# The down projection of an encoder layer: its operands made a third of a pair at a time, its partial sums loaded two at a time

## The chip, the cores and the metric

The kernel runs on one core of one Trainium2 chip. The metric is the device time of one execution in microseconds (us); less is better. The core has TensorE for matmuls (PE in the profile, its weight loads PEld), VectorE (DVE), ScalarE (ACT), GpSimd (POOL) and SyncE (SP); the last two and ScalarE also issue DMA transfers. Each engine works through its own queue in order, so an instruction that waits holds up all those behind it on the same engine.

## The reference

One layer of a hybrid encoder on a sequence of 512 tokens, width 2048, in float32. Behind a mixing stage (dilated attention and gated linear attention, not touched here) stands a SwiGLU with a hidden width of 5632:

```
h = rmsnorm(x, ffn_norm_w[l])
x = x + (jax.nn.silu(h @ w_gate[l]) * (h @ w_up[l])) @ w_down[l]
...
return rmsnorm(x, final_norm_w)
```

The change lies in the last product, by w_down (5632 x 2048).

## The kernel before

**Split operands.** A float32 operand is carried as two parts: `hi`, rounded by a cast on ScalarE, and `lo`, the rest, a subtraction on VectorE. Each product then takes three matmuls: hi x hi, hi x lo, lo x hi. So every weight that comes from memory costs a cast and a subtraction before TensorE can use it.

**Products of pairs.** A block of 2 x 2 tiles is multiplied by a scheme with seven products in place of eight. On the weights it needs sums (L1089 to L1091, VectorE), then the split of the loaded part and of the sums (casts L1101, subtractions L1106, two each). On the activations it needs, for each pair of 128-row tiles, sums and differences (L1323 to L1326) and their splits (L1335 to L1339, four casts and four subtractions). These are "the operands of a pair". The generator `operands` makes them and yields three times for each pair: behind L1326, behind the second split, and behind the fourth. So `make(1)` puts out a third of a pair and `make(3)` a whole one. A pair counts as made only with the call behind its last third, which begins the next pair too. The pair's raw tile is loaded by L1309 on SP from `gd`, where the gate and up stage had stored the activations; it starts a third only if enough buffers are free.

**Stages of w_down.** The 44 row tiles are dealt with in this order; the output has four blocks of 512 columns (c = 0 to 3):

1. Tiles 0 to 3 by plain products: four jobs, one for each block, of four halves each; a half is 12 matmuls of 512 columns (L293 to L295). Its weights are split at L196 and L197, three halves ahead. Before each half `before_down` runs (L1268), which calls `dn.make(3)`. Each job's result is added into `xd` in memory (L1262 on ScalarE, L1264 on POOL). In front of it `down_start` has made the first call of the generator, which loads two raw tiles.
2. Pairs 2 to 17 by the seven products (`Down`, L1286): 64 steps, ordered by chunk of pairs (2 to 7, 8 to 12, 13 to 17), within a chunk by block, within a block by pair. A step is 42 matmuls of 256 columns (L1374 to L1376), seven products of six. The pairs of a chunk are kept for its four blocks and their buffers are freed in its fourth. `run` (L1440) puts out, for step i: the load of weights (L1073, SP), the sums of step i + 2, the split of step i + 1, results that are still to be stored, then, while the step's pair is not made, `make(1)`; then the products, then `make(2)` and one call of `run_urgent`, which advances the first generator in the deque `urgent` to its next yield. At the last step of a block in a chunk the seven results go to `md` in memory: in the first chunk by plain stores from SP (L1398), later by adding stores from POOL (L1396).
3. When the last chunk has finished a block, `combine` (L1408) is put in `urgent`. It loads the block's seven sums from `md` (L1411, SP) and four tiles of the residual from `xd` (L1414, POOL), and some calls later adds them up in VectorE (L1422 to L1431) and into the residual (L1434).
4. Tiles 36 to 39 by plain products again: four jobs of four halves, 16 in all (`before_later`, L1474). A job's results are added to the residual by L1254, which frees the PSUM banks. Their splits run ever further ahead, so that at the end the weights of the next stage are split too. `run_side` advances `urgent` once behind each half but a job's last.
5. Tiles 40 to 43, the residual, the final norm and the stores (`finish`, L1514), in 16 groups of 12 matmuls (L1547 to L1549); `drain` ahead of it finishes whatever `urgent` still holds.

The order on each engine is the order in which the program puts instructions out; nothing reorders them. Buffers come from deques `s2` (70 of 512 columns), `s4` (16 of 1024) and `ps` (8 PSUM banks), the longest free one first, and whoever takes a buffer waits for its last reader.

Of the kernel before, what the change touches and what calls it, by code (L numbers as in the profile page):

```python
# [111 lines left out]
def put(*slots):  # L112
    for s in slots:
        if s.home is not None:
            s.home.free.append(s.i)


def layer(nc, tc, x, attn_norm_w, w_in, rel_table, gw_f, gb_f, gw_b, gb_b, gla_norm_w, w_out,
# [7 lines left out]
    with tc.manual_schedule(), \  # L126
# [5 lines left out]
        s2 = Slots(p2, N2, 512, "a")  # L132
# [22 lines left out]
        class Stream:  # L155
# [11 lines left out]
            def add(self, pieces):  # L167

                for segs in pieces:
                    self.pieces.append([segs, None])  # L170
                    for h in range(2):
                        self.halves.append([len(self.pieces) - 1, h, None, None])
# [52 lines left out]
        def run_urgent():  # L225
            while urgent:
                try:
                    next(urgent[0])
                    break
                except StopIteration:  # L230
                    urgent.popleft()
# [709 lines left out]
        x1 = {}  # L941
# [170 lines left out]
        class Feed(Blocks):  # L1112
# [80 lines left out]
            def run(self):  # L1193
                banks = {}
                for i, (u, q) in enumerate(self.seq):
                    if u not in banks:
                        banks[u] = [ps.get() for _ in range(4)]
                    self.load()
                    self.split(i)
                    self.sums(i + 1)  # L1200
                    self.sums(i + 2)
                    self.split(i + 1)
                    self.products(i, banks[u])
                    if u == len(self.units) - 1:
                        for p in (2 * q, 2 * q + 1):
                            put(*xs.pop(p)["slots"])
                        down_start(q)
                    for _ in range(3 if i < 8 else 1):
                        run_urgent()
                    if q == self.per - 1:  # L1210
                        urgent.append(self.evac(u, banks.pop(u)))
# [7 lines left out]
        def g_load(j):  # L1219
            if j < FF // 256 and j not in graw and 2 * j not in gT and j >= state["g"]:  # L1220
                state["g"] = j + 1
                graw[j] = s4.get(F32, [P, 2, 512])
                sp.dma_start(out=graw[j].t.rearrange("p f t -> p (f t)"), in_=gd[j])

        def g_split(j):
            if j in graw:
                r = graw.pop(j)
                for f in (1, 0):
                    hi, lo = s2.get(F32R), s2.get(F32R)
                    if f:  # L1230
                        act.activation(hi.t, r.t[:, f], AF.Copy, scale=-1.0)
                        dve.scalar_tensor_tensor(lo.t, r.t[:, f], -1.0, hi.f, op0=OP.mult, op1=OP.subtract)
                    else:
                        act.copy(hi.t, r.t[:, f])
                        dve.tensor_tensor(lo.t, r.t[:, f], hi.f, op=OP.subtract)
                    gT[2 * j + 1 - f] = (hi, lo)
                put(r)
# [30 lines left out]
        def before_down(c):  # L1268
            def f(i):
                if c == 0 and i == 0:  # L1270
                    g_split(1)
                dn.make(3)
                if c == 3:
                    dn.load()
                    if i >= 1:
                        dn.sums(i - 1)
                    if i == 2:
                        dn.split(0)
            return f
# [6 lines left out]
        class Down(Blocks):  # L1286
# [120 lines left out]

            def combine(self, c):  # L1408
                m = [s2.get(F32, [P, 2, 256]) for _ in range(7)]
                for n in range(7):  # L1410
                    sp.dma_start(out=m[n].t.rearrange("p s c -> p (s c)"), in_=md[7 * c + n])  # L1411
                x1[c] = [s2.get() for _ in range(4)]
                for t in range(4):
                    pool.dma_start(out=x1[c][t].t, in_=xd[4 * c + t])  # L1414
                for _ in range(3 if c < 3 else 5):
                    yield
                M = [None] + [x_.t for x_ in m]
                y = [s4.get(F32, [P, 2, 512]) for _ in range(2)]
                lo, up = slice(0, 256), slice(256, 512)
                add = lambda o, x_, y_: dve.tensor_tensor(o, x_, y_, op=OP.add)  # L1420
                sub = lambda o, x_, y_: dve.tensor_tensor(o, x_, y_, op=OP.subtract)
                add(y[0].t[:, :, up], M[2], M[1])  # L1422
                sub(M[3], M[1], M[3])
                yield
                sub(M[5], M[5], M[3])
                add(M[3], M[4], M[3])
                yield
                sub(y[0].t[:, :, lo], M[5], M[7])
                add(y[1].t[:, :, up], M[6], M[3])
                yield  # L1430
                sub(y[1].t[:, :, lo], M[5], M[4])  # L1431
                put(*m)
                for t in range(4):
                    dve.scalar_tensor_tensor(x1[c][t].t, y[t // 2].t[:, t % 2], rstd2[:, t:t + 1], x1[c][t].t,  # L1434
                                             op0=OP.mult, op1=OP.add)
                    if t % 2:
                        yield
                put(*y)

            def run(self):  # L1440
                for i, (ch, c, q) in enumerate(self.seq):
                    self.load()
                    self.sums(i)
                    self.split(i)
                    self.sums(i + 1)
                    self.sums(i + 2)
                    self.split(i + 1)
                    self.evac_late()
                    while q not in self.x:
                        self.make(1)  # L1450
                    self.products(i)
                    self.make(2)
                    run_urgent()
                    if ch == len(self.chunks) - 1 and c == 3:
                        n = self.chunks[ch].index(q)
                        if n == 0:
                            g_load(LAST // 2 - 2)
                        if n == 2:
                            g_split(LAST // 2 - 2)
                            g_load(LAST // 2 - 1)  # L1460
                            st.until, st.limit = None, 1
                            st.load()
                        if n > 2:
                            st.split(later_first + n - 2)
                self.evac_late()
                st.limit, st.big = 3, tail_first
# [7 lines left out]
        def before_later(c):  # L1474
            def f(i):
                j = LAST // 2 - 2 + (c + 1)
                if c and i == 0:
                    g_load(j)
                if i == (2 if c else 0) and c < 3:
                    g_split(j)  # L1480
            return f

        LAST = 40
# [11 lines left out]
        for c in range(4):  # L1495
            j = job("B", [piece512(w_down, c * 512, k) for k in (LAST - 4, LAST - 2)], list(range(LAST - 4, LAST)),
                    lambda k: gT[k], evac_later(c), before=before_later(c), rate=1.0)
            j.tail = c
            if c == 3:
                j.drop = drop_g  # L1500
        tail_first = len(st.halves)
        dn = Down([list(range(2, 8)), list(range(8, 13)), list(range(13, 18))])
# [94 lines left out]
```

## Time and profile before

| | us |
|---|---|
| median of 3 runs | 2249.7 |
| the runs | 2247.34 to 2252.29 |
| the profiled execution | 2248.97 |
| its span, first to last instruction | 2247.2 |
| TensorE busy in the span | 2213.8 |
| VectorE busy | 1633.1 |
| ScalarE busy | 1001.7 |
| stage 1 of w_down, first L293 to first L1374 | 1763.06 to 1817.30 |
| stage 2, first L1374 to the next L293 | 1817.30 to 2150.51 |
| stage 4, to the first matmul of stage 5 | 2150.51 to 2194.05 |

The page shows busy time by engine, then the span in 40 slices. Matmuls overlap and their ends are modelled, so busy time on PE is no measure of how much is lost; the distance between the starts of matmuls is. The chain of waits follows, from the last instruction back, what released each instruction; a line of it gives start, duration and what ran. The list of waits gives engine, line, what it waited for, then the total in us, the number of times and the longest one. A row of the table of stretches gives the stretch, its length, the busy time and number of instructions of PE, PEld, DVE, ACT and POOL, the granted clock of TensorE as a share of full speed, the busy share of the DMA engines and GB/s. A timeline gives start, duration, engine, line, what it writes and reads, and how many were merged.

### The profile page before, as it was taken

How to read it: one execution, taken by the hardware profiler on the slowest of the kernel's cores; microseconds unless marked ns; L12 is line 12 of the kernel's file. 1: busy time of each engine (PE TensorE's matmuls, PEld its weight loads, DVE VectorE, ACT ScalarE, POOL GpSimd, SP SyncE). 2: the span in 40 equal slices, each digit the busy share in tenths (PEclk: the TensorE clock that was granted, in tenths of full speed). 3: DMA queues.
4: the chain of work that ended last, by engine and by line, in shares of the span. 5: the costliest groups of instructions: out<-in, count | busy, mean ns of one | idle time of the engine just before them, and what ended most of it. 6: DMA issues, size and time to landing. Idle time of an engine off the chain costs nothing.

```text
span 2247.2 us, 37030 instructions
## 1 busy us (share of the span) xinstructions
PE 2213.8 (99%) x14814; PEld 2038.0 (91%) x14814; DVE 1633.1 (73%) x2717; ACT 1001.7 (45%) x1637; POOL 116.3 (5%) x173
## 2 busy tenths in 40 slices
PE   8999999999999999999999999999999899999998
PEld 6888887888888888999999999999999799999986
DVE  3366665745454446988888888888888877977777
ACT  5344444443444344434444343434444554655452
POOL 0000000000000100000000000000000110032220
PEclk9999999999999999999999999999999999999999
DMA  5525625232323432333333333333333764578993
GB/s 204 157 72 147 184 78 140 82 122 66 96 71 134 141 122 75 113 113 122 113 123 119 116 123 113 123 114 114 129 115 123 246 165 158 201 174 182 267 314 105
DMA packets 211805, 307.78 MB, mean 137 GB/s; under 512 B 15376, under 2 KB 131264, under 8 KB 211633
## 3 DMA queue, kind: packets, MB, share of 16 engines
q1 hardware_dynamic: 192480, 259.37, 35.9%
q0 software_dynamic: 18256, 44.99, 8.5%
q8 instruction: 116, 1.90, 0.3%
q10 hardware_dynamic: 896, 1.06, 0.1%
q14 instruction: 57, 0.46, 0.1%
HBM read 246.58 MB, written 46.20 MB: 130 GB/s over the span
## 4 chain that ended last, share of the span: by engine, by line
PE 92%; DVE 5%; ACT 1%; DMA 1%; issue 1%; SPq 0%; ACTq 0%; DVEq 0%
PE ps L1149 13%; PE ps L1148 13%; PE ps L1147 13%; PE ps L294 6%; PE ps L293 6%; PE ps L295 6%; PE ps L285 5%; PE ps L286 5%; PE ps L287 5%; PE ps L1375 4%; PE ps L1376 4%; PE ps L1374 4%; PE ps L514 1%; DVE b L1106 1%; DVE a L1339 1%; PE ps L841 1%
## 5 line engine op out<-in xcount | busy, mean ns | idle before, releaser
L1149 PE MATMUL ps<-a,b 128*128 128x256 f32 x2464 | 697.7, 283 | 2.9 <-DVE b L1106 2.9
L1147 PE MATMUL ps<-a,b 128*128 128x256 f32 x2464 | 697.4, 283 | 0.0
L1148 PE MATMUL ps<-a,b 128*128 128x256 f32 x2464 | 697.3, 283 | 0.0
L1101 ACT CAST b<-b 128x768 fp32r<-128x768 f32 x480 | 445.5, 943 | 550.8 <-DVE b L1106 318.8
L1106 DVE TENSOR_TENSOR b<-b,b 128x768 fp32r<-128x768 f32 x480 | 509.3, 1088 | 137.7 <-PE ps L1148 62.2
L1149 PEld LDWEIGHTS ps<-a,b 128*128 128x128 f32 x2464 | 473.0, 192 | 3.8 <-DVE b L1106 3.8
L1148 PEld LDWEIGHTS ps<-a,b 128*128 128x128 f32 x2464 | 473.0, 192 | 0.0
L1147 PEld LDWEIGHTS ps<-a,b 128*128 128x128 f32 x2464 | 473.0, 192 | 0.0
L197 DVE TENSOR_TENSOR a<-b,a 128x512 fp32r<-128x512 f32 x292 | 195.0, 686 | 135.8 <-ACT a L196 128.6
L1375 PE MATMUL ps<-b,a 128*128 128x256 f32 x896 | 255.2, 285 | 6.9 <-DVE b L1106 6.9
L1376 PE MATMUL ps<-b,a 128*128 128x256 f32 x896 | 254.3, 284 | 0.0
L1374 PE MATMUL ps<-b,a 128*128 128x256 f32 x896 | 254.2, 284 | 0.0
L196 ACT CAST a<-b 128x512 fp32r<-128x512 f32 x292 | 171.4, 617 | 53.1 <-DMA b<-in_w_in_dram 18.1
L293 PE MATMUL ps<-a,a 128*128 128x512 f32 x464 | 184.5, 398 | 2.5 <-ACT a L196 2.5
L294 PE MATMUL ps<-a,a 128*128 128x512 f32 x464 | 182.1, 392 | 4.4 <-DVE a L197 4.2
L295 PE MATMUL ps<-a,a 128*128 128x512 f32 x464 | 181.6, 391 | 0.0
L1375 PEld LDWEIGHTS ps<-b,a 128*128 128x128 f32 x896 | 172.6, 193 | 8.7 <-DVE b L1106 8.7
L1089 DVE TENSOR_TENSOR b<-b 128x512 f32<-128x512 f32 x240 | 164.0, 683 | 22.4 <-DMA b<-in_w_down_dram 18.5
L1374 PEld LDWEIGHTS ps<-b,a 128*128 128x128 f32 x896 | 172.7, 193 | 0.0
L1376 PEld LDWEIGHTS ps<-b,a 128*128 128x128 f32 x896 | 172.7, 193 | 0.0
L285 PE MATMUL ps<-a,a 128*128 128x512 f32 x416 | 168.3, 405 | 0.0
L286 PE MATMUL ps<-a,a 128*128 128x512 f32 x416 | 163.4, 393 | 0.0
(224 smaller groups left out, 3072.8 us busy)
## 6 DMA issues: line engine op xcount, KB each, us to landing
b<-in_w_gate_dram SPq DMA_DIRECT2D x88, 512.0 KB, 3.4
b<-in_w_up_dram SPq DMA_DIRECT2D x88, 512.0 KB, 3.5
b<-in_w_down_dram SPq DMA_DIRECT2D x88, 512.0 KB, 5.1
b<-in_w_in_dram SPq DMA_DIRECT2D x96, 256.0 KB, 4.4
b<-in_w_in_dram SPq DMA_DIRECT2D x48, 512.0 KB, 3.8
b<-in_w_out_dram SPq DMA_DIRECT2D x32, 512.0 KB, 4.1
md<-a POOLq DMA_DIRECT2D x56, 256.0 KB, 9.1
a<-a SPq DMA_DIRECT2D x96, 128.0 KB, 2.3
```

The costliest lines, as they stand in the source:

```text
L285: mm(o, wh.t[:, c], xh.t, start=first, stop=False)
L293: mm(o, xh.t[:, c], wh.t[:, w], start=first, stop=False)
L294: mm(o, xh.t[:, c], wl.t[:, w], start=False, stop=False)
L295: mm(o, xl.t[:, c], wh.t[:, w], start=False, stop=last)
L1101: act.copy(hi.t, src)
L1106: dve.tensor_tensor(lo.t, src, hi.f, op=OP.subtract)
L1147: mm(o, wh, xh, start=head, stop=False, skip_group_check=True)
L1148: mm(o, wh, xl, start=False, stop=False, skip_group_check=True)
L1149: mm(o, wl, xh, start=False, stop=end, skip_group_check=True)
L1374: mm(o, xh[:, t], wh, start=first and h == 0, stop=False, skip_group_check=True)
L1375: mm(o, xh[:, t], wl, start=False, stop=False, skip_group_check=True)
L1376: mm(o, xl[:, t], wh, start=False, stop=last, skip_group_check=True)
```

## The change

Four edits. In stage 1 one third of a pair is put out before each half where a whole pair was. In the steps one third is put out behind every second step, and behind every step of the fourth block, where two thirds were put out behind each. `combine` takes its buffers, waits a call (except for the last block), loads the sums of `md` two at a time with a call between, then the last one with the residual, and begins to add a call later (two for the last block). In stage 4 `run_urgent` is called once more, before each half.

```
@@ -1269,7 +1269,7 @@ before_down
                 if c == 0 and i == 0:
                     g_split(1)
-                dn.make(3)
+                dn.make(1)
                 if c == 3:
                     dn.load()
@@ -1407,12 +1407,17 @@
             def combine(self, c):
                 m = [s2.get(F32, [P, 2, 256]) for _ in range(7)]
+                x1[c] = [s2.get() for _ in range(4)]
+                if c < 3:
+                    yield
                 for n in range(7):
                     sp.dma_start(out=m[n].t.rearrange("p s c -> p (s c)"), in_=md[7 * c + n])
-                x1[c] = [s2.get() for _ in range(4)]
+                    if n in (1, 3, 5):
+                        yield
                 for t in range(4):
                     pool.dma_start(out=x1[c][t].t, in_=xd[4 * c + t])
-                for _ in range(3 if c < 3 else 5):
+                yield
+                if c == 3:
                     yield
                 M = [None] + [x_.t for x_ in m]
@@ -1449,7 +1454,8 @@ run
                     while q not in self.x:
                         self.make(1)
                     self.products(i)
-                    self.make(2)
+                    if c == 3 or i % 2:
+                        self.make(1)
                     run_urgent()
@@ -1478,6 +1484,7 @@ before_later
                 if i == (2 if c else 0) and c < 3:
                     g_split(j)
+                run_urgent()
             return f
```

More of the change, by code (lines that the diff above doesn't have):

```diff
@@ L1271, in f @@
                     g_split(1)
-                dn.make(3)
+                dn.make(1)
                 if c == 3:
@@ L1409, in combine @@
                 m = [s2.get(F32, [P, 2, 256]) for _ in range(7)]
+                x1[c] = [s2.get() for _ in range(4)]
+                if c < 3:
+                    yield
                 for n in range(7):
                     sp.dma_start(out=m[n].t.rearrange("p s c -> p (s c)"), in_=md[7 * c + n])
-                x1[c] = [s2.get() for _ in range(4)]
+                    if n in (1, 3, 5):
+                        yield
                 for t in range(4):
                     pool.dma_start(out=x1[c][t].t, in_=xd[4 * c + t])
-                for _ in range(3 if c < 3 else 5):
+                yield
+                if c == 3:
                     yield
@@ L1451, in run @@
                     self.products(i)
-                    self.make(2)
+                    if c == 3 or i % 2:
+                        self.make(1)
                     run_urgent()
@@ L1480, in f @@
                     g_split(j)
+                run_urgent()
             return f
```

## The prediction

> **What bounds the kernel now.** I read the first part of the page, then the waits of the stretch from 1740 us on, then single stages. I call the 64 rounds of L1374 to L1376 (42 matmuls each) steps 0 to 63; the 16 rounds of 12 matmuls ahead of them (stage 1) are halves 0 to 15.
>
> ```profile
> PE 2213.8 (99%) x14814; PEld 2038.0 (91%) x14814; DVE 1633.1 (73%) x2717; ACT 1001.7 (45%) x1637; POOL 116.3 (5%) x173
> ```
>
> ```profile
> PE ps L1375 <- DVE b L1106: 6.9, 8, 3.2
> PE ps L294 <- DVE a L197: 4.2, 4, 1.1
> PE ps L293 <- ACT a L196: 2.5, 2, 1.5
> ```
>
> TensorE is the bound; behind the gate stage it waits only for splits of weights. These waits understate the loss (ends are modelled), so I use starts. Without waiting, matmuls start 0.12 us (256 wide) or 0.227 us (512 wide) apart: stage 4, the twin of stage 1 with 192 matmuls, runs from 2150.51 to 2194.05, 43.5 us or 2.72 a half; stage 1 takes from 1763.06 to 1817.30, 54.2. **10.7 us are lost there.** The 2688 matmuls of the steps last from 1817.30 to 2150.51, 333.2 us, against 64 x 5.04 = 322.6: **10.6 us lost**, by starts of steps 0.25 in step 1, 4.4 in 24 to 28, 1.06 in 42 and 43, 4.99 in step 53. The tail loses nothing. So 21.3 us is all that can be won.
>
> Stage 1, in its chain of waits:
>
> ```profile
> 1778.72 0.33 DVE a L1323
> 1779.05 0.34 DVE a L1324
> 1779.39 0.35 DVE a L1325
> ...
> 1779.76 0.42 DVE a L1326
> 1780.19 0.34 DVE a L1336
> 1780.52 1.81 DVE a L1339 x3
> 1782.33 0.60 DVE a L197
> ```
>
> A whole pair of operands (L1323 to L1339) is 3.6 us of VectorE, and the weight split L197, which TensorE waits for, stands behind it: 4.2 us a half against 2.72. Steps 24 to 28 have the same cause. Step 53 has another:
>
> ```profile
> 2072.10 13.15 DMA md<-a
> 2085.26 0.32 SPq L1411
> 2085.69 0.38 SPq L1073
> ...
> 2086.68 5.90 DMA b<-in_w_down_dram
> 2092.59 0.96 DVE b L1106
> 2093.59 0.43 PE ps L1375
> 2070.80 14.78 SPq L1411 DMA_DIRECT2D a<-md  x7
> ```
>
> Seven loads of sums hold SP for 14.8 us while the adding stores land, and weights (L1073) queue behind. The last row is SP's timeline.
>
> Two stretches at half clock complete it; the column after POOL is the clock:
>
> ```profile
> 1783.20:1786.60 3.40, 3.40 (x9) 2.63 (x9) 3.37 (x9) 3.40 (x8) 2.62 (x3) 0.50 1.07 160
> 2093.80:2097.20 3.40, 3.40 (x17) 3.40 (x17) 3.33 (x6) 2.49 (x4) 0.00 (x0) 0.50 0.04 12
> ```
>
> Each costs half of its 3.4 us, 1.7, and is inside the sums above.
>
> **The change, part by part.** Matmuls keep their order and number; copies, sums and transfers keep their number. Only places in queues move.
>
> *One third instead of three in stage 1.* Thirds are 1.45 (L1323 to L1326), 0.94 (L1336, one L1339) and 1.2 us (two L1339). VectorE reaches the first at 1762.6. Half by half it then has 2.0, 2.3 (with L1158, L1166), 3.5 (three L1158) and 3.2 us (L1188), so the splits that halves 3 to 6 need are ready near 1764.6, 1766.9, 1770.4 and 1773.6, against 1771.2, 1773.9, 1776.7 and 1779.4. Later 1.5 to 2.0 a half against 2.72. ScalarE's casts with them (0.62 each, 0.43 for L1335) are 1.7 to 1.9 a half, up to 4.6 where four L1262 (0.68) fall, every fourth half, within a lead of three halves. Gain 10.7; step 1's 0.25 too, since no third's cast stands ahead of L1262 there. If transfers were late instead (L196 waited for one 10.5 us from 1740 on), part stays, at most half.
>
> *Thirds beside the steps.* Five pairs and a third come out of stage 1 instead of eight; the rest of the 16 is made in the steps. A saturated step costs VectorE 2.0 (two L1106), 1.47 (L1089 to L1091) and now at most 1.45, 4.9 against 5.04: no backlog grows. Before, two thirds at once gave 5.8 to 6.2. Gain 4.4 + 1.06.
>
> *What is late next.* Thirds come in every second step for three column blocks of four, so two pairs are not ready and are forced: in steps 28 and 48 the last third stands in the queue behind the split of the next step, though TensorE wants it now, in its 15th matmul, 14 x 0.12 = 1.68 us after the step's start. In an ordinary step that split is done 2.43 after the start (the sums start at 1900.60, step 16 at 1898.17); two L1339 (1.29) make 3.72: 2.0 late. In step 28 the first cast waits for the last matmul of step 27 (buffers), some 0.7 more; in step 48 a forced third ahead (step 47) and 0.94 and 1.47 behind it give 2.43 + 1.34 + 0.94 + 1.47 = 6.18, 1.14 into the step, and 1.14 + 2.0 + 1.29 = 4.43: 2.75 late. Both together 3.4 (splits without any wait) to 5.8; I take **5.4**.
>
> *The clock then.* Half clock came at 1783.2 after some 2.5 us idle out of 3.4, in pieces of at most 1.4, and at 2093.8 after 3.4 in one. It did not come after 1.65 idle (1774.4 to 1776.1) nor in steps 24 to 28 (at most 1.15 each). The new waits of 2.7 lie nearer to the first kind, if they fall into one window: none to two, 0 to 3.4 us. I take one, **1.7**. [...]
>
> *Sums loaded two at a time.* They start a step later and take four steps. On SP numbers 0 and 1 issue behind the L1073 of step 50, 0.6 into it, 10.7 us after step 48 began; the adding stores that they read had landed 8 us after it (SP's second L1411). The last load issues 25.8 after it, against 20.4 (2085.26). Margins 2.7 and 5.4, so nothing holds SP. The four loads on POOL now precede three late adding stores, 2 us, which nobody awaits. Gain 4.99, bounds 0 and 4.99. The additions (0.6 each, the last four 0.66) fall on steps with no thirds left: 3.47 + 1.3.
>
> *Stage 4.* The additions of block 1 slide into it, and more calls bring those of block 3 ahead of its last weight splits. Before, VectorE did 37.7 us of work and waited 6.4 for weights between 2153.3 and its first L1254 of the last block at 2197.55; now 6 x 0.6 more for block 1 and 7 x 0.6 + 4 x 0.66 = 6.8 for block 3, 48.1. That L1254 then ends 2.8 + 48.1 + 0.7 = 51.6 into the stage, and the fifth group of the tail needs its bank at 43.5 + 4 x 2.72 = 54.4. Margin 2.8; of the 6.4 us the extra 3.6 ahead hides as much, and 1 MB more is loaded. Bounds 0 and 3.6; I take **1**.
>
> *Sum:* 2248.97 (the profiled execution; its span is 2247.2, 1.8 lies around it) - 10.7 - 0.25 - 5.46 - 4.99 + 5.4 + 1.7 + 1 = 2235.7. The profiled execution is 0.7 under the median, 2249.7, inside the runs' own spread of 5; I leave it so: **2236**.
>
> **The rivals.**
> - [...] Chance 0.25. [...]
> - *The sums still hold SP*: three more stores or loads nearby could slow the landing beyond the 2.7 us margin; it spread from 4 to 13 us in one group. Up to 5 back: 2241. Chance 0.12.
> - *VectorE late at the tail*: as before, DMA is busy all of 2150 to 2172. Each microsecond waited beyond 2.8 is one of TensorE: the old 6.4 in full gives 3.6, and a half clock behind it 1.7, in place of my 1: 2240. Chance 0.12.
> - *Stalls only move* (the change does not do what it says): thirds and sums at 4.9 of 5.04 leave 0.1, and waits for casts make a backlog in steps 19 to 24 and 40 to 48 as large as the old 5.5, beside a stage 1 bound by transfers (5 stay): 2246. Chance 0.06.
> - *Slower:* SP's weight loads behind the operands' own buffer. In nine steps a load of weights takes the buffer that the middle third has just read (before, L1073 waited 52.6 us in 9 such cases, 22.1 the longest). From a load's usual turn, the start of a step, 5.04 + 2.43 = 7.5 us remain to its sums, and it takes 5.1 to land (the table of issues), so it decides once that L1339 ends over 2.4 us after a step's start; then each of nine costs some 3 us of idle, near the 3.4 of step 53: 2236 + 9 x 3 = 2263. Against it: that third ends some 2.43 + 0.94 = 3.4 into the step before, 1.6 ahead of the load's turn. Chance 0.05.
>
> **How the numbers follow.** Forecast 0.40. The range from 2230 (waits at 3.4, no half clock, nothing at the tail: 2231) to 2244 (5.8, 3.4, 3.6 and part of a kept wait) leaves out the last two rivals and some of the others' ends. About 0.2%, 4.5 us, is what a measurement tells from no change. Faster 0.89 (the first four cases), within it 0.06, slower 0.05.
>
> **What would show it.** Stage 1 lasts 43.5 us; steps 24 to 27, 42, 43 and 53 take 5.04; steps 28 and 48 take some 7.7, waiting in matmul 15 for L1339; half clock follows one of them; SP's loads of sums issue without a wait for md; tail groups 4 and 5 start at most a microsecond late. Wrong it is if weights are awaited from transfers in stage 1, or if steps 29 on stay over 5.04.

## The result, and the profile after

The changed kernel takes **2238.72 us** (median of 5 runs, 2237.59 to 2239.87), the kernel before beside it 2248.36 (5 runs, 2247.12 to 2252.29): a ratio (of the means) of **0.9954**, 95% interval 0.994 to 0.9969. The profiled execution took 2238.72 us too, its span 2236.9. Up to L1407 the line numbers are those of before; then the loads of sums are L1414, those of the residual L1418, the additions L1423 to L1436 and L1439.

The first part of the page shows nothing but the shorter span: every engine does the work that it did.

```profile
PE 2210.6 (99%) x14814; PEld 2037.6 (91%) x14814; DVE 1635.0 (73%) x2717; ACT 1002.4 (45%) x1637; POOL 115.8 (5%) x173
```

The waits of TensorE from 1740 us to the end (engine, line, what it waited for; total us, times, longest) are a different list from that of before:

```profile
PE ps L1376 <- DVE a L1339: 3.6, 2, 2.7
PE ps L294 <- DVE a L197: 2.1, 1, 2.1
PE ps L1374 <- ACT a L1338: 1.5, 1, 1.5
```

L1375 no longer waits for L1106. What is left are operands of a pair (L1338, L1339) and one wait of L294, which is in stage 4. By starts of matmuls, with the loss counted against what each part takes without any wait (43.55 for a stage of 16 halves, 322.56 for the 64 steps):

| us | before | after | lost after, and where |
|---|---|---|---|
| first matmul of stage 1 | 1763.06 | 1761.99 | |
| stage 1 | 54.24 | 43.55 | nothing |
| steps | 333.21 | 329.89 | 7.3: step 28 takes 9.45, step 48 7.97, all others 5.04 |
| stage 4 | 43.55 | 48.35 | 4.8: halves 2, 3, 5 and 6 take 3.07, 3.13, 6.11 and 3.37 for 2.72 |
| tail, first to last matmul | 43.29 | 43.29 | nothing |

Stage 1 and the steps gained 14.0 us, stage 4 gave 4.8 back. The first row's 1.07 is not the change's: all kernels of this study are the same up to there, and their stage 1 begins between 1760.95 and 1763.06.

Stage 1 in four stretches of four halves (stretch, length, busy us of PE, PEld, DVE, ACT, POOL, clock, DMA share, GB/s):

```profile
1761.99:1772.88 10.89, 10.89 (x50) 9.01 (x49) 10.42 (x21) 4.82 (x9) 1.36 (x3) 1.00 1.02 387
1772.88:1783.77 10.89, 10.89 (x49) 9.01 (x48) 7.10 (x14) 7.52 (x15) 3.60 (x6) 1.00 1.01 286
1783.77:1794.66 10.89, 10.89 (x50) 9.01 (x49) 8.71 (x18) 7.77 (x15) 3.47 (x6) 1.00 0.79 147
1794.66:1805.54 10.88, 10.88 (x50) 9.01 (x49) 9.32 (x17) 7.43 (x13) 3.57 (x6) 1.00 0.63 98
```

PE is busy for the whole of each stretch, though the DMA share is 1.02 and 1.01 in the first two: VectorE, with 10.42 of 10.89 in the first, just keeps up, and no transfer is late.

### The profile page after: what moved, and what is told of

Read it like the earlier page. It is cut to its first block, busy times and chain, and to the rows that moved or that the text cites. A ratio compares the mean times of both kernels' runs of the same rounds, so it can differ in the third digit from the quotient of the medians.

```text
span 2236.9 us, 37003 instructions
## 1 busy us (share of the span) xinstructions
PE 2210.6 (99%) x14814; PEld 2037.6 (91%) x14814; DVE 1635.0 (73%) x2717; ACT 1002.4 (45%) x1637; POOL 115.8 (5%) x173
## 3 DMA queue, kind: packets, MB, share of 16 engines
q10 hardware_dynamic: 896, 1.06, 0.1%
## 4 chain that ended last, share of the span: by engine, by line
PE 88%; issue 6%; POOL 2%; DMA 1%; DVE 1%; ACT 1%; SPq 0%; POOLq 0%; ACTq 0%; DVEq 0%
PE ps L1149 13%; PE ps L1148 13%; PE ps L1147 13%; PE ps L294 6%; PE ps L295 6%; PE ps L293 6%; PE ps L285 5%; PE ps L286 5%; PE ps L287 5%; PE ps L1376 2%; PE ps L1375 2%; PE ps L1374 2%; POOL md L1396 2%; PE ps L514 1%; PE ps L841 1%
## 5 line engine op out<-in xcount | busy, mean ns | idle before, releaser
L1101 ACT CAST b<-b 128x768 fp32r<-128x768 f32 x480 | 445.5, 942 | 537.5 <-DVE b L1106 284.8
L1106 DVE TENSOR_TENSOR b<-b,b 128x768 fp32r<-128x768 f32 x480 | 510.2, 1089 | 139.2 <-PE ps L1148 62.5
L197 DVE TENSOR_TENSOR a<-b,a 128x512 fp32r<-128x512 f32 x292 | 195.0, 686 | 125.5 <-ACT a L196 122.8
L1375 PE MATMUL ps<-b,a 128*128 128x256 f32 x896 | 254.2, 284 | 0.0
L294 PE MATMUL ps<-a,a 128*128 128x512 f32 x464 | 182.0, 392 | 2.3 <-DVE a L197 2.1
L293 PE MATMUL ps<-a,a 128*128 128x512 f32 x464 | 184.1, 397 | 0.0
L1375 PEld LDWEIGHTS ps<-b,a 128*128 128x128 f32 x896 | 172.8, 193 | 0.0
```

Source lines behind the costliest of these rows:

```text
L293: mm(o, xh.t[:, c], wh.t[:, w], start=first, stop=False)
L294: mm(o, xh.t[:, c], wl.t[:, w], start=False, stop=False)
L1101: act.copy(hi.t, src)
L1106: dve.tensor_tensor(lo.t, src, hi.f, op=OP.subtract)
L1375: mm(o, xh[:, t], wl, start=False, stop=False, skip_group_check=True)
```

## What was asked of the experiments

Three losses were left: step 28, step 48 and stage 4. The first theory for stage 4 was this: the additions of block 1 now stand in VectorE's queue ahead of the weight splits of half 5, and they wait for the residual. The chain that ended last in 2135:2165 has it (start, duration, what):

```profile
2136.00 0.53 POOL a L1418
2136.53 14.36 DMA a<-xd
2151.19 0.21 issue
2151.58 0.70 DVE a L197
2152.32 0.50 PE ps L294
```

The residual, issued at 2136.53, landed 14.36 us later; then comes L197, and only then L294. (The chain leaves out the addition L1439 between them; the list of waits in 2126:2184 has it as "DVE a L1439 <- DMA a<-xd: 2.9, 3, 1.5".) The rival: not the late transfer but the added call in stage 4 does it, which puts additions ahead of splits whatever they wait for.

## The parts alone

**Stage 1 alone.**

```
-                dn.make(3)
+                dn.make(1)
```

> The kernel before with only the edit of stage 1: a third before each half instead of a whole pair; the steps still put out two thirds behind each, the sums are loaded all at once. Theory (the whole loss of stage 1 is whole pairs ahead of the weight splits): stage 1 takes 43.5 us as in the changed kernel; the pairs not made there are made in steps 1 to 4, where two thirds for four steps stay within the slack; steps 24 to 28, 42, 43 and 53 lose the same 10.4 us as before; time 2248.4 - 10.7 - 0.2 = 2237.5, as fast as the whole change. Rival (stage 1 was freed only because the steps took thirds singly, or because weights came earlier): steps 1 to 8 lose 3 us or more, time 2240 or above.

Measured: 2238.19 us, ratio 0.9953 (0.9936 to 0.9969): as fast as the whole change. Stage 1 takes 43.55; the steps take 333.54, with steps 24 to 28 at 5.67 to 6.19 and step 53 at 9.59; stage 4 and the tail lose nothing. Steps 4 and 5 take 5.59 and 5.67, which they did not before: the pairs that stage 1 no longer makes cost 1.2 us there, where the expectation had nothing. All of TensorE's waits from 1740 us on are on one line:

```profile
PE ps L1375 <- DVE b L1106: 6.9, 9, 2.8
```

It is the first row of before (6.9, 8, 3.2) but for one wait more and a shorter longest one: this edit takes out the rows of L293 and L294. So the other three edits together added nothing to it that can be measured.

**The sums' edits alone** (all of `combine` and the call in stage 4, below only the places where calls come in; operands as before).

```
...
+                if c < 3:
+                    yield
                 for n in range(7):
                     sp.dma_start(...)
+                    if n in (1, 3, 5):
+                        yield
...
+                run_urgent()
```

> The kernel before with only the edits of the sums: two loads at a time, and the additional calls in stage 4; pairs are made as before. Theory (late residual tiles cost stage 4 its 4.8 us, whatever the operands do): step 53 takes 5.04 (5.0 won), stage 4 takes about 48 (4.8 lost), stage 1 and steps 24 to 28 as before; time 2248.2, no change. Rival (stage 4 lost because the other edits brought it forward or changed its buffers): stage 4 takes 43.5 and the time is 2243.4.

Measured: 2248.87 us, ratio 0.9999 (0.999 to 1.0009). Step 53 takes 5.04, so its 4.99 is won; stage 4 takes 49.09, so 5.5 is lost, in the same halves 2, 3, 5 and 6 as in the whole change. With stage 1's operands as before, the loss in stage 4 is still there: it belongs to the sums' edits.

**The operands' edits alone** (`make(1)` in stage 1, thirds in every second step; sums as before).

```
-                    self.make(2)
+                    if c == 3 or i % 2:
+                        self.make(1)
```

> The kernel before with the two edits of the operands alone (one third in stage 1, one third in every second step and in every step of the fourth block); combine and stage 4 as before. Computes all that the reference does. Theory (of 10.7 won in stage 1 all stays; the thirds win 5.46 in steps 24 to 28, 42 and 43 and lose 5.5 in the waits of steps 28 and 48, with a half clock of 1.7 where one window holds more than 1.7 idle; step 53 keeps its loss of 5; stage 4 has no loss): 2236.5 to 2240, no faster than stage 1 alone (2238.2). Rival (the waits of steps 28 and 48 come from how the sums' edit moved VectorE's work, and go without it): 2232 to 2234.

Measured: 2236.14 us, ratio 0.9941 (0.9929 to 0.9954). Step 28 takes 7.95, step 48 9.45 (7.97 in the whole change), and TensorE's waits hold the two rows of the whole change unaltered:

```profile
PE ps L1376 <- DVE a L1339: 3.6, 2, 2.7
PE ps L1375 <- DVE b L1106: 1.7, 1, 1.7
PE ps L1374 <- ACT a L1338: 1.5, 1, 1.5
```

The waits of steps 28 and 48 thus come from the thirds, not from the sums. The middle row is step 53, which lost only 2.0 here; the expectation had it keep its 5.0, and the 3.0 less bring this kernel slightly under the expected 2236.5. That half clock follows where one window holds more than 1.7 idle was the author's estimate; no run shows such an edge. Nothing is lost in stage 4.

## The forced thirds

Two more thirds, so that the two pairs are not short of one:

```
-                    if c == 3 or i % 2:
+                    if c == 3 or i % 2 or i in (26, 46):
```

> The changed kernel with one more third behind steps 26 and 46, so that the last pairs of chunks 2 and 3 are ready in time; all else as in the changed kernel. Theory (steps 28 and 48 wait only for the forced last third): both take 5.04, no half clock follows step 28, 4.4 + 2.9 us won: 2238.7 - 7.3 = 2231.4. Rival (VectorE has a backlog there in any case): the loss moves to steps 27 to 29 and 47 to 50 and the time stays at 2236 or above.

Measured: 2235.15 us (2230.9 to 2235.62), ratio 0.9932 (0.9917 to 0.9947). Step 28 is at 5.04. Step 48 still takes 7.08: its pair was short of two thirds, and one remains. So the cause of step 28 is shown; step 48 loses 2.0 in place of 2.9, so its cause is shown only in part, and a later kernel (below) adds a third at 44 and cures it. The profiled execution is the 2230.9, the fastest by 4.1; more on this in the last section.

## Stage 4

**The residual loaded first** (whole change, the loads L1418 moved behind the first two sums):

```
+                    if n == 1:
+                        for t in range(4):
+                            pool.dma_start(out=x1[c][t].t, in_=xd[4 * c + t])
                     if n in (1, 3, 5):
                         yield
-                for t in range(4):
-                    pool.dma_start(out=x1[c][t].t, in_=xd[4 * c + t])
```

> The changed kernel with the four residual tiles of a block loaded with its first two sums, three calls earlier than in the changed kernel; all else as there. Theory (in stage 4 the additions of block 1 wait for residual tiles that POOL issued behind four adding stores, and the weight splits stand behind them): stage 4 takes 43.5, 4.8 us less: 2233.9; steps 28 and 48 stay. Rival (the weights themselves are late, since all DMA engines are busy): halves 2 to 6 of stage 4 still lose 3 us or more, 2237 or above.

Measured: 2240.11 us, ratio 0.9958 (0.9943 to 0.9973): nothing won. Half 5 is cured, but halves 2 and 11 take 3.99 and 4.95, and the tail loses 1.8. In 2126:2200 the additions now wait for sums, and a bank comes free late:

```profile
DVE a L1427 <- DMA a<-md: 5.2, 1, 5.2
...
PE ps L293 <- DVE a L1254: 2.1, 1, 2.1
```

**The first theory fell.** It named the right wait for half 5, but to load the residual earlier only makes the sums the late ones: the load for which L1427 waits took 18.96 us, from 2145.41 to 2164.37. In the whole change the residual took 14.36, with a DMA share of 1.08 meanwhile (2136.53:2150.89): the additions wait for a late transfer in both kernels, for the residual there, for a sum here.

**Sums of blocks 1 to 3 at once, with and without the added call.** Two kernels that differ in that call alone: both keep the pacing for block 0 and load the other blocks as before.

```
-                if c < 3:
+                if c == 0:
                     yield
...
-                    if n in (1, 3, 5):
+                    if c == 0 and n in (1, 3, 5):
                         yield
...
-                yield
-                if c == 3:
+                for _ in range((1, 3, 3, 5)[c]):
                     yield
```

The second leaves out `run_urgent()` in `before_later` too.

> The changed kernel, but only block 0 loads its sums two at a time; blocks 1 to 3 load all seven and the residual in one call, with the waits of the kernel before. The additional calls in stage 4 stay. Loading the residual earlier did not help: the additions then waited for sums that took 19 us to land in a stretch with all DMA engines busy. Theory now: what block 1 loads in the steps (step 60) instead of in stage 4 lands in time, so halves 2 to 6 lose nothing from it; block 2's loads may still be waited for, up to 2 us: stage 4 takes 43.5 to 45.5, time 2234 to 2236. Rival (the additional calls are the cause: additions stand ahead of splits whatever is loaded when): stage 4 stays at 47 or above, 2238.

> As the run before, and without the additional calls in stage 4, so that additions and splits there take turns as in the kernel before, two calls later. Theory (late transfers under additions that stand ahead of splits): stage 4 takes 43.5, the tail as before, time 2238.7 - 4.8 = 2233.9. Rival (weights are late there because transfers moved into stage 4 in any case): 46 or above, 2236.5.

Measured: **2249.06** us (ratio 0.9996, 0.9987 to 1.0005) with the call and **2241.78** (ratio 0.9965, 0.9951 to 0.9978) without it. With the call stage 4 takes 49.25 and the tail loses 2.8; without it they take 43.55 and 43.29, no loss at all. In this pair of kernels the call alone costs stage 4 its time. TensorE's waits from 2080 us on with the call, the three largest:

```profile
PE ps L1553 <- DVE a L1254: 4.0, 1, 4.0
PE ps L1374 <- ACT b L1101: 3.1, 1, 3.1
PE ps L294 <- DVE a L197: 0.8, 1, 0.8
```

The place is another than in the whole change: halves 5 and 6 lose nothing here, halves 2 and 3 lose 1.5, and half 15 loses 4.2, where the tail's first bank waits for L1254. So the pair shows that the call puts additions ahead of work that TensorE waits for; that it makes half 5 of the whole change wait is argued from the chain there. All twelve kernels bear it out: the five with the call lose 3.1 to 5.7 in stage 4, the seven without it at most 0.6.

Without the call, from 1740 us on, the rows of L1254 and L197 are gone and one that is second in the list above leads:

```profile
PE ps L1374 <- ACT b L1101: 4.2, 1, 4.2
```

That is steps 62 and 63, which take 9.38 and 7.89: the price of loading block 1 at once. Its eleven transfers go out at step 59, and ScalarE, where the cast L1231 of a tile for stage 4 stands ahead of the weight cast L1101, waits in 2110:2150:

```profile
ACT a L1231 <- DMA b<-gd: 13.9, 1, 13.9
```

So the theory that pacing blocks 1 to 3 was needless failed as well: pacing block 1 is right, the added call is wrong. The whole change without the call alone was not tried: by a count of calls, block 3's residual buffers would then be taken too late.

Without the call something is lost behind these stages: from the start of the last matmul to the end of the kernel it is 10.92 us, against 9.87 in the whole change. The last kernel below has the same loss, and its chain shows where.

## Towards a better version

**Old calls, and three more thirds** (26, 44 and 46).

> As the run before, and one more third behind steps 26, 44 and 46, since with 26 and 46 alone the last pair of the last chunk was still short by one third and step 48 kept 2 us. Theory: all steps take 5.04 and all stages are without loss: 2248.4 - 21.4 = 2227. Rival (something else becomes late, by the half clock or VectorE's backlog in steps 44 to 48, where a third falls in every step): 2229.5 or above.

Measured: 2233.79 us, ratio 0.9928 (0.9916 to 0.9941). Every step but 62 and 63 takes 5.04, step 48 among them: its idle is shown to be that of the forced thirds. Those two still lose 5.3, which the expected 2227 left out.

**One more call in each step of block 1**, to bring the sums of block 1 forward:

```
                     run_urgent()
+                    if ch == len(self.chunks) - 1 and c == 1:
+                        run_urgent()
```

> As the run before, and two calls of the urgent work behind each step of the last chunk's second block (steps 53 to 57), so that block 0 is added up in half the steps and block 1 loads two steps sooner. Theory (VectorE has room for two additions more in a step once no thirds are left: 3.47 + 2.4 = 5.9 for two steps, within a slack of some 4): no loss, 2227, same as the run before. Rival (a backlog): steps 55 to 60 lose 1 to 3 us, 2229.

Measured: 2236.78 us, ratio 0.9939 (0.9924 to 0.9955). The expectation names the wrong steps; by the edit the second call falls in steps 49 to 53. The sums of block 0 then load two steps earlier, before their adding stores have landed, and the seven of block 1 behind them hold SP for 15.06 us from 2082.94 on. SP's waits in 2055:2110:

```profile
SPq L1414 <- DMA md<-a: 22.4, 12, 3.1
```

Steps 53, 55 and 58 take 8.65, 6.31 and 9.25; 62 and 63 are cured. Loading earlier is worth nothing if the load must wait on SP.

**Block 1 paced too**, its residual behind its first two sums, one extra call in step 57 so that it begins a step earlier; old calls in stage 4, thirds as above. In part, against the kernel with three more thirds:

```
                if c == 0:
                    yield
                for n in range(7):
                    sp.dma_start(...)
+                    if c == 1 and n == 1:
+                        for t in range(4):
+                            pool.dma_start(out=x1[c][t].t, in_=xd[4 * c + t])
-                    if c == 0 and n in (1, 3, 5):
+                    if c < 2 and n in (1, 3, 5):
                         yield
...
                    run_urgent()
+                    if i == 57:
+                        run_urgent()
```

> The kernel with the old calls in stage 4 and three more thirds, and now the sums of block 1 loaded two at a time as well (its residual behind the first two), beginning one step earlier, at the end of step 58, by one more call at step 57; the loads then lie in steps 58 to 61. Computes all that the reference does. Theory (steps 62 and 63 lost 5.3 us there because eleven transfers of block 1, put out at once at step 59, filled the DMA engines while weights and a tile for stage 4 were awaited): both steps at 5.04, or 0 to 2 us lost in them; stage 1, stage 4 and tail without loss: 2227 to 2229. Rival (the DMA engines are full over steps 58 to 63 whatever the order, 0.98 to 1.05 busy from 2110 to 2150, so the loss stays or moves by some steps): 2231 to 2235.

Measured: **2229.25 us** (2228.71 to 2229.75), ratio **0.991** (0.9895 to 0.9925), 9.5 us under the change. Stage 1, steps and stage 4 in three stretches:

```profile
1762.18:1805.73 43.55, 43.55 (x195) 36.05 (x193) 35.54 (x70) 27.51 (x49) 12.00 (x15) 1.00 0.88 229
1805.73:2128.28 322.55, 322.55 (x2690) 322.55 (x2688) 272.50 (x416) 179.88 (x256) 51.27 (x63) 1.00 0.76 207
2128.28:2172.41 44.13, 43.85 (x195) 35.97 (x194) 34.29 (x56) 22.74 (x41) 11.76 (x18) 1.00 1.02 334
```

PE's busy time is the length of the stretch in the first two: 64 steps without a wait. All that is left of TensorE's waiting behind 1740 us is one row, 0.58 us by starts, in half 2 of stage 4:

```profile
PE ps L294 <- DVE a L197: 0.3, 1, 0.3
```

Of the 21.3 us that the prediction gave as the most to be won, the span shows 20.3 (2247.2 - 2226.9). Stage 1 and the steps give 21.35, all of it, and stage 1 began 0.88 earlier; stage 4 takes back 0.58, and the end of the kernel 1.39. From the start of the last matmul to the end it is 11.24, against 9.85 before, and the chain that ended last runs there through VectorE, not through TensorE:

```profile
2213.42 0.67 DVE a L1254
2214.11 0.69 DVE a L1565
2214.80 0.67 DVE a L1254
```

VectorE ends block 3's additions 17.6 us into the tail here (2190.05), against 13.3 before (2207.37), and it does not catch up: at the end of this kernel VectorE is the bound.

DMA moves no less than before: in 2110:2130, most of steps 60 to 63, its share is 1.06 here and was 0.98 two kernels earlier, with 16.60 us of PE in the 20. It was when the loads were put out, not their amount.

## Why the prediction was right, and where it was not

The forecast was 2236, its sum 2235.7 against 2238.72 measured in the profiled execution. Step by step:

- **Stage 1**, 10.7 and step 1's 0.25: 10.69 came, and step 1 is at 5.04. VectorE's work was forecast at 11.0 in the first four halves (10.42 measured) and at 1.5 to 2.0 a half later; the table above has 1.8, 2.2 and 2.3, nearer to the limit of 2.72 than thought, without reaching it.
- **Thirds beside the steps**, 4.4 + 1.06: steps 24 to 27, 42 and 43 are at 5.04. No backlog grew.
- **What is late next**, 5.4: measured 1.63 + 1.08 in step 28 and 2.83 in step 48, 5.5 in all, against 2.7 and 2.75. In step 28 TensorE waits twice: 1.63 first for the cast L1338 in matmul 13, then 1.08 for L1339 in matmul 15, where the text had the whole of it. Chance has a part in so close a sum; that the steps and the cause are right, two kernels show (26 added: step 28 cured; 44 and 46 added: step 48).
- **The clock**, one half clock, 1.7: behind these two waits one came, in step 28, a clock of 0.50 in 1952.42:1955.84 (the other one of this trace, in stage 4, is counted below). That it was one, and there, is partly chance. Of five kernels that keep both waits, step 28 alone takes 9.45 in two, step 48 alone 9.45 and 9.47 in two, and both are lengthened in one. The chance of 0.25 was that of no half clock at all; it did not hold here: the 3.41 us ahead of the half clock, with PE busy for 1.78, hold parts of two gaps of 1.63 and 1.08. That it takes a wait inside one window was the author's estimate, which no run shows as a rule.
- **Sums**, 4.99: step 53 is at 5.04. In 2060:2110 SP waits for nothing but buffers, not for md:

```profile
SPq L1073 <- PE ps L1376: 32.2, 7, 8.2
SPq L1073 <- PE ps L1375: 17.6, 4, 4.6
```

- **Stage 4**, 1: this is **the term that was mis-sized**, 4.8 measured. The step added up VectorE's work from the start of the stage to the bank that the tail needs. That sum was not wrong: the L1254 in question, forecast to end 51.6 behind the start of the stage, starts 54.9 behind it, in a stage grown by 4.8, and the tail lost nothing. But it was made for one point only. The calls that bring block 3's additions ahead of the last splits also bring block 1's ahead of the splits of half 5, where the queue has no 2.8 us of slack. The wait of TensorE there is 2.27, the half clock behind it (0.50 in 2153.81:2157.22) 1.7, and halves 2 and 3 lose 0.76: 4.8. The rival "VectorE late at the tail" had the price (2240) and the engine, but the same wrong place; it came true in another kernel, where the tail's first bank waits 4.0 for L1254 (sums at once, with the call).
- **SP behind the operands' buffer**, the rival on the slower side, did not come: no step but 28 and 48 is over 5.04.

The rest is small: 3.8 us of stage 4 and 0.3 of the steps, less the 1.07 by which stage 1 begins earlier (chance, not the change), make the 3.0 between 2235.7 and 2238.72.

What the parts alone add is what the prediction's sum does not show: the gain of the whole change is that of its first edit. The thirds win 5.5 and lose about as much in steps 28 and 48, more where one of them takes 9.45 in place of 7.95 or 7.97; the sums win 5.0 in step 53 and lose 4.8 in stage 4.

## What to carry to other kernels

When an edit advances a side job by more calls, check each point at which its instructions now enter the queue of an engine, with the slack there, and not only the sum of the work up to the last deadline. Pacing a producer down is free until the first consumer that is short by one piece: count the pieces for every consumer, since one missing third cost 2.7 us, and three well-placed ones won all of it back. And take a change of several edits apart: here one line gave as much as all four. The others became worth 9 us only when three thirds were added, the sums were paced anew and the call in stage 4 was left out.

## What the runs showed of the hardware

**Half clock in the whole change.** From 1740 us to the last matmul the granted clock was 0.50 in two stretches of 3.41 us, one in step 28 and one in stage 4. Each stands here below the 3.41 us ahead of it; the last two rows are those of step 48 (busy times with modelled ends):

```profile
1949.01:1952.42 3.41, 1.78 (x12) 1.57 (x13) 3.38 (x7) 2.12 (x5) 1.75 (x2) 1.00 0.35 19
1952.42:1955.84 3.42, 3.42 (x18) 3.42 (x17) 1.58 (x4) 1.41 (x3) 1.75 (x2) 0.50 0.94 161
2150.40:2153.81 3.41, 1.49 (x7) 1.24 (x7) 2.90 (x5) 0.63 (x1) 0.98 (x2) 1.00 1.10 265
2153.81:2157.22 3.41, 3.41 (x10) 2.64 (x9) 3.41 (x6) 1.14 (x2) 0.73 (x3) 0.50 1.06 356
2051.41:2054.82 3.41, 2.29 (x20) 2.08 (x18) 3.34 (x6) 1.18 (x2) 1.16 (x2) 1.00 0.49 154
2054.82:2058.23 3.41, 1.86 (x15) 1.86 (x16) 2.95 (x6) 0.95 (x2) 0.80 (x2) 1.00 1.00 130
```

PE was busy for 1.78 and 1.49 of 3.41 ahead of the two stretches at 0.50. The longest wait of all, the 2.83 of step 48, lies in the last two rows, with 2.29 and 1.86 busy, and the clock was 1.00 there and in 2058.23:2061.65 behind them. In the operands' edits alone PE was busy for 0.75 in 2052.08:2055.50, with the same 2.83 in step 48, and the step took 9.45 in place of 7.97. How much idle time it takes for half clock to follow, the runs do not show.

**One kernel, two times.** With two more thirds the profiled execution took 2230.9 us and the other three 2234.99 to 2235.62. In its trace TensorE waits 1.94 in step 48 and 2.19 in half 5 of stage 4, and the mean granted clock is 0.999. The other three were not traced, but theirs is 0.998. As an estimate, one stretch of 3.41 us at 0.50, like those above, takes 0.0008 off the mean over 2229 us, so these rounded means differ by about one such stretch: 1.7 of the 4.1 to 4.7. The trace of the 2230.9 also has the earliest start of stage 1 of all twelve (1760.95; the others 1761.67 to 1763.06). What makes up the rest is open.

**Landing times.** In the whole change a residual tile took 14.36 us to land in stage 4, with a DMA share of 1.08 meanwhile, where the table of issues has a median of 9.9 for them; a load of sums took up to 19.7 (median 10.4 for 21 loads from 2065 to 2145).
